# Forget gates inside the first stage, four projection chunks ahead of attention, two branch weights and gate chunks at its end, zero rows from another tile

## The chip, the core and the metric

The kernel runs on one core of a Trainium2 chip. Its time is the device time of one execution in microseconds (us), and lower is better. The core has five engines that run their own instruction streams: TensorE (PE, with its weight loads as PEld), VectorE (DVE), ScalarE (ACT), GpSimd (POOL) and SyncE (SP), which here issues nearly all DMA transfers. Each engine takes its instructions in the order in which they stand in its stream; semaphores order the streams against each other.

## What is computed

One layer of an encoder block on 1024 tokens of width 1024, all in float32:

```
z   = rms_norm(x) @ W_in          # q/k/v + forget logits (8), q/k/v of the second attention, 2 x 1024 gates
a   = forgetting attention         # 8 heads of 64, causal; scores + F_q - F_k, F = cumsum(log_sigmoid(ff + b))
b   = differential attention       # 4 heads, two score sets each, bias of distance, rms_norm of the result
y   = sigmoid(g_a) * (a @ W_pa) + sigmoid(g_b) * (b @ W_pb)
x   = x + y @ W_o
x   = x + two-of-32 expert layer(rms_norm(x))
out = rms_norm(x)
```

Every float32 matrix product is made of three matmuls: each operand is split into a high part, rounded to the matmul's format, and the low rest, and hi·hi, hi·lo and lo·hi are summed in PSUM.

## The kernel before

Five stages follow one another, and what matters here is how they meet.

- **Stage 1** (`stage_z1`, to about 118 us): norm of the eight token tiles, transposes, then the value columns and the forget logits in four column chunks (`values(c, t)`, c = 0..3; the logits come with c = 1). `stage_forget` follows as a piece of its own: log-sigmoid on ACT and DVE, a cumulative sum over tokens as twelve matmuls `pf` against a triangle `tri`, the result `t1` stored to the scratch tensor `fscr`. Its tiles are in pools that open after stage 1's have closed.
- **Projection chunks** (`z2_chunk`): 32 chunks of 128 columns, in the order q/k of the first attention (8), q/k of the second (8), gates (16). A chunk loads its weights (`zraw`), splits them (`zhi` on ACT, `zlo` on POOL), and makes 16 *pieces* of three matmuls into `pz`. After each half of a chunk ACT and DVE evict it (`sh`, `sl`) and four DMAs write q or k to scratch; gates get one. `fill(n)` emits n pieces. The first 2 chunks (32 pieces) run ahead of attention.
- **Attention** (`pipeline`): 8 heads of the first kind, then 4 of the second, eight query tiles (steps) each. A step makes scores (`ps`), DVE adds the bias and takes the maximum (`te`), ACT exponentiates, DVE scales, PE transposes (`pt`), ACT and DVE evict the transposed probabilities as high and low part (`PT`), PE multiplies with the values (`po`). Pieces of the projection are spread between these as filling, by weight i + 1.5 for step i: 256 in all for the first kind, 224 for the second.
- **Branches** (`branches(hb)`, from about 740 us): the attention outputs come back from scratch (`o`), the two branch weights are loaded in eight column groups (`praw`), split (`phi`, `plo`), multiplied (`pj`), gated, summed; then the output product, norm and routing by tiles.
- **Experts** (from about 981 us): 32 experts whose weights are streamed, and the final norm.

Around the change the PE order is the program's own (`manual_schedule`) from the first projection chunk to the end of attention. The other engines' streams, SP's among them, and PE's in stage 1 and in the branches are set by a list scheduler when the program is built, which takes instructions by priority as soon as its own clock says that they are ready; a DMA can thus stand far ahead of its place in the program. The zero rows of `ys` (2048 rows into which the experts' results are scattered) are one such case: `ys_clear` stands after attention in the program, its 16 DMAs from the tile `zero` stand in SP's stream in stage 1, from 37.6 to 77 us.

Buffers come from pools that are stacked; a tile of a new pool waits for the old tiles whose place it takes.

Of the kernel before, what the change touches and what calls it, by code (L numbers as in the profile page):

```python
# [8 lines left out]
F32 = mybir.dt.float32  # L9
# [42 lines left out]
class Block:  # L52
# [77 lines left out]
    def stage_z1(self):  # L130
# [4 lines left out]
        with ExitStack() as st:  # L135
# [67 lines left out]
            for t in range(NT):  # L203
                norm(t)
                if t + 4 < NT:
                    load_x(t + 4)
                if t == 3:
                    nc.sync.dma_start(self.bff, self.bcast(a["b_fgate"]))
                    load_w(1)
                values(0, t)  # L210
            for c in range(1, 4):
                if c + 1 < 4:
                    load_w(c + 1)
                for t in range(NT):
                    values(c, t)


    def stage_forget(self):
        nc = self.nc
        self.fscr = self.dram("fscr", [FOX_H, S], F32)  # L220
        with ExitStack() as st:
            p = self.pool(st, "fg")
            pp = self.pool(st, "pfg", space=PSUM)
            x = self.ffall.rearrange("p t h -> p (t h)")
            n = NT * FOX_H
            ab = p.tile([128, n], F32, name="ab")
            nc.scalar.activation(ab, x, AF.Abs)
            nc.scalar.activation(ab, ab, AF.Exp, scale=-1.0)
            nc.scalar.activation(ab, ab, AF.Ln, bias=1.0)
            lf = p.tile([128, n], F32, name="lf")  # L230
            nc.vector.scalar_tensor_tensor(lf, x, 0.0, ab, op0=OP.min, op1=OP.subtract)
            st_ = p.tile([128, NT, 64], F32R, name="lfs")
            nc.vector.memset(f32(st_), 0.0)
            l3 = lf.rearrange("p (t h) -> p t h", t=NT)
            nc.vector.tensor_copy(st_[:, :, 0:8], l3)
            nc.vector.tensor_tensor(st_[:, :, 32:40], l3, f32(st_[:, :, 0:8]), op=OP.subtract)
            ji = p.tile([128, S], I32, name="ji")
            nc.gpsimd.iota(ji, pattern=[[1, S]], base=0, channel_multiplier=-1)
            tri = p.tile([128, S], F32R, name="tri")
            nc.vector.tensor_scalar(tri, ji, 0.0, None, op0=OP.is_ge)  # L240
            ps = pp.tile([64, S], F32, name="pf")
            for hb in range(2):
                js = [j for j in range(NT) if j * 128 < (hb + 1) * 512]
                for j in js:
                    k0 = max(hb * 512, j * 128)
                    nc.tensor.matmul(ps[:, k0:(hb + 1) * 512], st_[:, j], tri[:, k0 - j * 128:(hb + 1) * 512 - j * 128],
                                     start=(j == 0), stop=(j == js[-1]))
            t1 = p.tile([8, S], F32, name="t1")
            nc.scalar.activation(t1, ps[32:40], AF.Copy)
            nc.vector.scalar_tensor_tensor(t1, ps[0:8], -1.0, t1, op0=OP.mult, op1=OP.subtract)  # L250
            nc.sync.dma_start(self.fscr, t1)


    def z2_setup(self, st):
# [9 lines left out]
        self.zero = self.pool(st, "zz", side="right").tile([128, 512], F32, name="zero")  # L264
        self.nc.gpsimd.memset(self.zero, 0.0)
# [57 lines left out]
    def z2_all(self):  # L323
# [6 lines left out]
        self.fill(2 * 2 * KC)  # L330
# [247 lines left out]

    def proj_setup(self, sa, sb, sw):
# [3 lines left out]
        self.opp = self.pool(sa, "op", 1)  # L583
        self.wpp = self.pool(sa, "wp", 2)
        self.tpp = self.pool(sa, "tpp", 2)
# [33 lines left out]

    def branches(self, hb):  # L620
# [3 lines left out]
        O = [self.opp.tile([128, KC, 512], F32R, name=f"o{s}") for s in range(2)]  # L624
        for br_ in range(2):
            for s in range(2):
                nc.sync.dma_start(f32(O[s][:, 4 * br_:4 * br_ + 4]),
# [636 lines left out]
```

## Time and profile before

| | |
|---|---|
| median of 3 runs | 1620.63 us (1620.57 to 1621.64) |
| profiled execution | 1615.66 us, span 1613.8 us |
| PE busy | 1493.0 us, 93% of the span |
| DVE, ACT, POOL busy | 1048.1, 882.5, 288.8 us |
| mean granted PE clock | 0.971 |
| stage 1 / chunks and forget / attention | to 118.5 / to 158.2 / to 722.5 us |
| gap and branches, first half | 722.5 to 740.0 / to 786 us |

A row of the timeline is start, duration, engine, line, operation, output<-input, shape and count; in brackets stands how long the engine had been idle before it, and what it waited for. `L305` is line 305 of the kernel. PEclk is the share of the full TensorE clock that was granted. A row of windows has the stretch, its length, the busy time (with the number of instructions) of PE, PEld, DVE, ACT and POOL, then PEclk, the share of DMA and GB/s.

### The profile page before, as it was taken

What the parts mean: (1) busy time and instruction counts of PE and PEld (TensorE: products, weight loads), DVE (VectorE), ACT (ScalarE), POOL (GpSimd) and SP (SyncE); (2) the same over time, 40 slices, a digit from 0 to 9 for tenths busy, and PEclk for the clock granted to TensorE, in tenths of its full rate; (3) what the DMA queues carried; (4) which work ended last, traced back from release to release, by engine and by line L of the source; (5) the groups of instructions that cost most, each with busy time, mean ns of one, the idle gap of its engine ahead of it and who ended that gap; (6) DMA issues with size and microseconds to landing.
All of it is one profiled execution on the core that took longest, in us unless ns stands there. A gap on an engine that the chain in (4) does not pass through costs nothing.

```text
span 1613.8 us, 21890 instructions
## 1 busy us (share of the span) xinstructions
PE 1493.0 (93%) x7713; PEld 1174.4 (73%) x7713; DVE 1048.1 (65%) x1926; ACT 882.5 (55%) x1327; POOL 288.8 (18%) x278
## 2 busy tenths in 40 slices
PE   6996999999999999996999959999999998999996
PEld 6994777777788888885888846666667666666663
DVE  6112555555555545545657459999999888888966
ACT  5212444444454444433312138878888877777764
POOL 2301122222221321210020131131011111111014
PEclk9998999999999999998999979999999999999998
DMA  8927566666644544349934759999999999999936
GB/s 267 332 96 236 139 179 171 164 161 162 159 134 129 166 151 131 111 148 248 313 112 144 313 202 337 377 354 368 385 376 375 374 344 356 346 350 342 351 133 253
DMA packets 181284, 394.94 MB, mean 245 GB/s; under 512 B 21714, under 2 KB 99538, under 8 KB 156594
## 3 DMA queue, kind: packets, MB, share of 16 engines
q1 hardware_dynamic: 174114, 376.89, 69.3%
q0 software_dynamic: 7056, 16.62, 3.1%
q8 instruction: 61, 1.00, 0.3%
q14 instruction: 53, 0.43, 0.1%
HBM read 324.36 MB, written 77.25 MB: 249 GB/s over the span
## 4 chain that ended last, share of the span: by engine, by line
PE 79%; DVE 8%; DMA 6%; issue 4%; ACT 2%; SPq 1%; POOL 1%; ACTq 0%; DVEq 0%; POOLq 0%
PE pz L305 7%; PE pz L306 7%; PE pz L307 7%; PE m L980 6%; PE m L981 6%; PE m L979 6%; PE mpy L1013 3%; PE mpy L1011 3%; PE mpy L1012 3%; DVE mlo L46 3%; PE po L472 2%; PE pt L386 2%; PE ps L360 2%; PE ps L361 2%; DMA mraw<-in_w_dram 2%
## 5 line engine op out<-in xcount | busy, mean ns | idle before, releaser
L46 DVE TENSOR_TENSOR mlo<-mraw,mhi 128x1024 fp32r<-128x1024 f32 x384 | 450.1, 1219 | 40.5 <-ACT mhi L45 38.7
L45 ACT ACTIVATE mhi<-mraw 128x1024 fp32r<-128x1024 f32 x384 | 391.7, 1056 | 64.3 <-PE m L981 46.6
L980 PE MATMUL m<-mlo,XT 128*96 128x512 f32 x512 | 205.6, 402 | 22.3 <-DVE mlo L46 22.3
L305 PE MATMUL pz<-ht,zhi 128*128 128x512 f32 x512 | 215.6, 421 | 0.0
L979 PE MATMUL m<-mhi,XT 128*96 128x512 f32 x512 | 206.5, 403 | 0.0
L981 PE MATMUL m<-mhi,XT 128*96 128x512 f32 x512 | 205.1, 401 | 0.0
L307 PE MATMUL pz<-ht,zlo 128*128 128x512 f32 x512 | 202.5, 396 | 0.0
L306 PE MATMUL pz<-ht,zhi 128*128 128x512 f32 x512 | 201.3, 393 | 0.0
L369 ACT ACTIVATE te<-te,nm 128x256 f32<-128x256 f32 (+7 forms) x128 | 99.2, 775 | 145.1 <-DVE nm L365 145.1
L980 PEld LDWEIGHTS m<-mlo,XT 128*96 128x96 f32 x512 | 84.3, 165 | 64.8 <-DVE mlo L46 31.0
L365 DVE CUSTOM_DVE_ANT_0 te<-ps,nF 128x512 f32<-128x512 f32 (+3 forms) x128 | 75.0, 588 | 76.8 <-PE ps L361 48.6
L46 DVE TENSOR_TENSOR PT<-pt,PT 128x512 fp32r<-128x512 f32 (+1 forms) x144 | 77.0, 554 | 73.3 <-ACT PT L45 71.4
L277 POOL TENSOR_TENSOR zlo<-zraw,zhi 128x1024 fp32r<-128x1024 f32 x32 | 76.7, 2398 | 209.9 <-ACT zhi L276 208.9
L307 PEld LDWEIGHTS pz<-ht,zlo 128*128 128x128 f32 x512 | 96.7, 189 | 21.9
L45 ACT ACTIVATE PT<-pt 128x512 fp32r<-128x512 f32 (+1 forms) x144 | 66.4, 488 | 84.2 <-PE pt L386 57.6
L981 PEld LDWEIGHTS m<-mhi,XT 128*96 128x96 f32 x512 | 84.1, 164 | 35.4 <-issue 0.5
L979 PEld LDWEIGHTS m<-mhi,XT 128*96 128x96 f32 x512 | 84.3, 165 | 34.4 <-issue 0.6
L305 PEld LDWEIGHTS pz<-ht,zhi 128*128 128x128 f32 x512 | 98.4, 192 | 13.5
L306 PEld LDWEIGHTS pz<-ht,zhi 128*128 128x128 f32 x512 | 97.7, 191 | 13.6
L1013 PE MATMUL mpy<-mhi,GT 128*96 128x512 f32 x256 | 101.7, 397 | 2.8 <-DVE GT L46 2.5
L1011 PE MATMUL mpy<-mhi,GT 128*96 128x512 f32 x256 | 102.3, 400 | 0.6 <-ACT GT L45 0.6
L1012 PE MATMUL mpy<-mlo,GT 128*96 128x512 f32 x256 | 100.4, 392 | 0.0
(263 smaller groups left out, 2797.1 us busy)
## 6 DMA issues: line engine op xcount, KB each, us to landing
mraw<-in_w_dram SPq DMA_DIRECT2D x192, 1024.0 KB, 8.1
zraw<-in_w_in_dram SPq DMA_DIRECT2D x32, 512.0 KB, 4.3
ys<-zero SPq DMA_DIRECT2D x16, 512.0 KB, 4.9
gscr<-sh SPq DMA_DIRECT2D x32, 256.0 KB, 2.0
o<-oscr SPq DMA_DIRECT2D x8, 1024.0 KB, 7.5
g<-gscr SPq DMA_DIRECT2D x32, 256.0 KB, 4.5
mraw<-ys SPq DMA_DIRECT2D x8, 1024.0 KB, 10.9
xt<-in_x_dram SPq DMA_DIRECT2D x8, 512.0 KB, 5.0
```

The source lines that it names most:

```text
L45: nc.scalar.activation(hi, src, AF.Copy)
L46: nc.vector.tensor_tensor(lo, src, f32(hi), op=OP.subtract)
L305: nc.tensor.matmul(ps, hi[:, k], self.hT[0][:, k, tk], start=(k == 0), stop=False)
L306: nc.tensor.matmul(ps, hi[:, k], self.hT[1][:, k, tk], start=False, stop=False)
L307: nc.tensor.matmul(ps, lo[:, k], self.hT[0][:, k, tk], start=False, stop=(k == KC - 1))
L369: nc.scalar.activation(t[:, :n], t[:, :n], AF.Exp, scale=-1.0, bias=nm, accum_out=rs)
L979: nc.tensor.matmul(ps, XT[0][:, k], hi, start=(k == 0), stop=False)
L980: nc.tensor.matmul(ps, XT[0][:, k], lo, start=False, stop=False)
L981: nc.tensor.matmul(ps, XT[1][:, k], hi, start=False, stop=(k == KC - 1))
L1011: nc.tensor.matmul(ps[n], GT[0][:, k], hi[:, nn], start=(k == 0), stop=False)
L1012: nc.tensor.matmul(ps[n], GT[0][:, k], lo[:, nn], start=False, stop=False)
L1013: self.last_down = nc.tensor.matmul(ps[n], GT[1][:, k], hi[:, nn], start=False, stop=(k == 3))
```

## The change

Five things move.

1. `stage_forget` becomes a generator inside stage 1, with stage 1's pools. Its first half (log-sigmoid, the triangle, now 640 wide) is emitted after `values(2, 0)`, its second (the matmuls in two groups, eviction in two halves, the store to `fscr`) after `values(2, 4)`. The cleared `lfs` moves from DVE to POOL.
2. 64 pieces (4 chunks) run ahead of attention in place of 32.
3. The filling of attention is 224 pieces for the first kind and 200 for the second; the 24 pieces that are left stand after attention.
4. Attention's pools close when its pipeline ends. Then `proj_first` opens the pools of the branch weights and loads the weights of the first two column groups and the first part of `o`, ahead of the 24 pieces in the program.
5. The zero rows come from `yroom` (cleared at setup by POOL) in whole 4 KB rows, emitted four each in the norm of the tiles 0 to 3; the tile `zero` is gone.

```
-            self.stage_forget()
-            self.att_setup(st)
             with self.tc.manual_schedule(engines={mybir.EngineType.PE}):
-                self.z2_all()
...
-                self.pipeline(share(fox, 16 * KC * 2 - 4 * KC + 32) + share(diff, 14 * 2 * KC))
-                self.fill(16 * KC)
-            self.ys_clear()
+                with ExitStack() as sh:
+                    self.att_setup(sh)
+                    self.z2_all()
...
+                    self.pipeline(share(fox, 14 * 2 * KC) + share(diff, 12.5 * 2 * KC))
+                sa = ExitStack()
+                self.proj_first(sa)
+                self.fill(2 * 2 * KC)
...
-        self.fill(2 * 2 * KC)
+        self.fill(4 * 2 * KC)
...
+            forget = self.stage_forget(gp, pp)
             for c in range(1, 4):
...
                 for t in range(NT):
                     values(c, t)
+                    if c == 2 and t in (0, 4):
+                        next(forget)
...
+    def proj_first(self, sa):
+        self.wpp = self.pool(sa, "wp", 2)
+        self.opp = self.pool(sa, "op", 1)
+        self.tpp = self.pool(sa, "tpp", 2)
+        self.bw = {j: self.branch_weights(j) for j in range(2)}
+        self.O = self.branch_rows()
+        self.load_o(0, 0)
...
+    def branch_weights(self, j):
+        nc, a = self.nc, self.a
+        n = slice(j * 128, (j + 1) * 128)
+        raw = self.wpp.tile([128, KC, 128], F32, name="praw")
+        hi = self.wpp.tile([128, KC, 128], F32R, name="phi")
+        lo = self.wpp.tile([128, KC, 128], F32R, name="plo")
+        nc.sync.dma_start(raw[:, 0:4], a["w_pa"][0].rearrange("(c p) n -> p c n", p=128)[:, :, n])
+        nc.sync.dma_start(raw[:, 4:8], a["w_pb"][0].rearrange("(c p) n -> p c n", p=128)[:, :, n])
+        split(nc, hi, lo, raw)
+        return hi, lo
...
+        if t < NT // 2:
+            for i in range(4):
+                self.ys_clear(4 * t + i)
...
-        nc.vector.memset(f32(st_), 0.0)
+        nc.gpsimd.memset(f32(st_), 0.0)
...
-        tri = p.tile([128, S], F32R, name="tri")
+        tri = p.tile([128, 640], F32R, name="tri")
...
-    def ys_clear(self):
+    def ys_clear(self, t):
-        self.ys = self.dram("ys", [2 * S, D], F32)
-        for t in range(2 * NT):
-            self.nc.sync.dma_start(self.ys[t * 128:(t + 1) * 128].rearrange("p (k n) -> p k n", k=2),
-                                   self.zero.unsqueeze(1).to_broadcast([128, 2, 512]))
+        self.nc.sync.dma_start(self.ys[t * 128:(t + 1) * 128], self.yroom)
```

How the streams move, at three places.

SP's stream from the store of the forget sums to the first load of `kk` (the keys of head 0), before: the store waits for `t1` and stands ahead of the keys, with parts of q and the values between.

```order
L275 DMA zraw<-in_w_in_dram 128x8x128
L399 DMA qq<-qscr_f 128x512
L251 DMA fscr<-t_1388 8x1024
L401 DMA qq<-qscr_f 64x512
L402 DMA qq<-qscr_f 64x512
L456 DMA v<-vscr_f 128x8x128
L392 DMA kk<-kscr_f 128x1024
```

Now the store (L255) stands in stage 1, among the stores of the values, and the keys of head 0 come after the stores of the third chunk's first half, while a chunk and a half of matmuls are still ahead of attention:

```order
L322 DMA kscr_f<-sh 64x512
L323 DMA kscr_f<-sl 64x512
L453 DMA nF<-fscr 128x1024
L322 DMA qscr_f<-sh 64x512
L323 DMA qscr_f<-sl 64x512
L322 DMA qscr_f<-sh 64x512
L323 DMA qscr_f<-sl 64x512
L395 DMA kk<-kscr_f 128x1024
```

What moved is the store, out of the way of the keys, and the four stores of one more half chunk, ahead of them.

ACT's stream where the first head gives way to the second (`te` 128x1024 is the last step's exponential, `te` 128x128 the next head's first), before:

```order
L369 ACTIVATE te,rs<-te,nm 128x1024
L45 ACTIVATE PT_1915<-pt 128x3x128
L45 ACTIVATE PT_1914<-pt 128x4x128
L276 ACTIVATE zhi<-zraw 128x1024
L369 ACTIVATE te,rs<-te,nm 128x128
L45 ACTIVATE sh<-pz 128x512
L45 ACTIVATE PT_1914<-pt 128x4x128
L45 ACTIVATE PT_1915<-pt 128x4x128
```

and now:

```order
L372 ACTIVATE te,rs<-te,nm 128x1024
L45 ACTIVATE sh<-pz 128x512
L45 ACTIVATE PT_2038<-pt 128x3x128
L45 ACTIVATE PT_2037<-pt 128x4x128
L372 ACTIVATE te,rs<-te,nm 128x128
L45 ACTIVATE PT_2037<-pt 128x4x128
L45 ACTIVATE PT_2038<-pt 128x4x128
```

The split `zhi` and the eviction `sh` have left this place. Before, 32 pieces per head put a chunk's end at every change of heads, and all seven changes read alike. With 28 pieces the place wanders: the changes 1, 2, 5 and 6 have no `zhi` there, 3 and 7 have it ahead of the `PT` evictions, and the fourth, like the change to the second attention, reads as before. On PE one piece in place of two stands between the last head's transposes and the new head's first.

ACT's stream at the end of attention, now (`PT` of the last two query tiles, which the last products wait for):

```order
L372 ACTIVATE te,rs<-te,nm 128x1024
L412 ACTIVATE ohi<-ot 128x512
L45 ACTIVATE phi<-praw 128x1024
L45 ACTIVATE PT_7346<-pt 128x3x128
L45 ACTIVATE phi<-praw 128x1024
L45 ACTIVATE PT_7345<-pt 128x4x128 x2
L45 ACTIVATE PT_7346<-pt 128x4x128
```

and SP's at the same place:

```order
L637 DMA praw<-in_w_pa_dram 128x4x128
L638 DMA praw<-in_w_pb_dram 128x4x128
L637 DMA praw<-in_w_pa_dram 128x4x128
L415 DMA oscr_1387<-ohi 128x512
L415 DMA oscr_1388<-olo 128x512
L638 DMA praw<-in_w_pb_dram 128x4x128
```

Before, both `phi` stood after the last `PT` and the last `ohi`, and no load of `praw` stood ahead of the store of that `olo`. Now the two splits stand between the last evictions (the two `plo` likewise on DVE), and the second weights' second half is issued after the store of `olo`, the low part of the output of the half before the last; on POOL a `zlo` has come to stand ahead of that `olo`. The 16 stores of zero rows stand in SP's stream between the second and the sixth head of the first attention.

More of the change, by code (lines that the diff above doesn't have):

```diff
@@ L215, in stage_z1, with stage_forget @@
                     values(c, t)
-    def stage_forget(self):
+                    if c == 2 and t in (0, 4):
+                        next(forget)
+    def stage_forget(self, p, pp):
         nc = self.nc
         self.fscr = self.dram("fscr", [FOX_H, S], F32)
[L221 to L232, printed above, removed]
-            nc.vector.memset(f32(st_), 0.0)
[L234 to L238, printed above, removed]
-            tri = p.tile([128, S], F32R, name="tri")
[L240 to L251, printed above, removed]
@@ new lines, in stage_forget @@
+        x = self.ffall.rearrange("p t h -> p (t h)")
+        n = NT * FOX_H
+        ab = p.tile([128, n], F32, name="ab")
+        nc.scalar.activation(ab, x, AF.Abs)
+        nc.scalar.activation(ab, ab, AF.Exp, scale=-1.0)
+        nc.scalar.activation(ab, ab, AF.Ln, bias=1.0)
+        lf = p.tile([128, n], F32, name="lf")
+        nc.vector.scalar_tensor_tensor(lf, x, 0.0, ab, op0=OP.min, op1=OP.subtract)
+        st_ = p.tile([128, NT, 64], F32R, name="lfs")
+        nc.gpsimd.memset(f32(st_), 0.0)
@@ new lines, in stage_forget @@
+        l3 = lf.rearrange("p (t h) -> p t h", t=NT)
+        nc.vector.tensor_copy(st_[:, :, 0:8], l3)
+        nc.vector.tensor_tensor(st_[:, :, 32:40], l3, f32(st_[:, :, 0:8]), op=OP.subtract)
+        ji = p.tile([128, 640], I32, name="ji")
+        nc.gpsimd.iota(ji, pattern=[[1, 640]], base=0, channel_multiplier=-1)
+        tri = p.tile([128, 640], F32R, name="tri")
+        nc.vector.tensor_scalar(tri, ji, 0.0, None, op0=OP.is_ge)
+        yield
+        t1 = p.tile([8, S], F32, name="t1")
@@ new lines, in stage_forget @@
+        for hb in range(2):
+            ps = pp.tile([128, 4, 128], F32, name="pt", bufs=4).rearrange("p a b -> p (a b)")[:64]
+            js = [j for j in range(NT) if j * 128 < (hb + 1) * 512]
+            for j in js:
+                k0 = max(hb * 512, j * 128)
+                w, o = (hb + 1) * 512 - k0, min(k0 - j * 128, 128)
+                nc.tensor.matmul(ps[:, k0 - hb * 512:], st_[:, j], tri[:, o:o + w], start=(j == 0), stop=(j == js[-1]))
+            c = slice(hb * 512, (hb + 1) * 512)
+            nc.scalar.activation(t1[:, c], ps[32:40], AF.Copy)
+            nc.vector.scalar_tensor_tensor(t1[:, c], ps[0:8], -1.0, t1[:, c], op0=OP.mult, op1=OP.subtract)
@@ L254, in z2_setup @@
+        nc.sync.dma_start(self.fscr, t1)
+        yield
     def z2_setup(self, st):
@@ L1220, in run @@
                 sw = sb.enter_context(ExitStack())
-                with ExitStack() as sa:
+                with sa:
                     self.proj_setup(sa, sb, sw)
```

37 lines of the change are left out of this document (17 added, 20 removed).

## The prediction

> **What bounds the kernel now.** I read the page first, then PE's waits, then the windows around the longest of them, then the timeline at both ends of attention.
>
> ```profile
> span 1613.8 us, 21890 instructions
> PE 1493.0 (93%) x7713; PEld 1174.4 (73%) x7713; DVE 1048.1 (65%) x1926; ACT 882.5 (55%) x1327; POOL 288.8 (18%) x278
> ```
>
> PE is busy for 93% of the span, so a gain is either PE work that disappears, and this change removes none worth the name, or PE time that is waited away or runs at a reduced clock. The waits of PE, where the columns are the sum in us, the count and the longest:
>
> ```profile
> PE pt L386 <- DVE PT L46: 15.3, 8, 2.2
> PE pj L644 <- ACT phi L45: 12.5, 1, 12.5
> PE ps L360 <- DMA kk<-kscr_f: 10.2, 1, 10.2
> PE pf L246 <- DVE lfs L236: 5.4, 1, 5.4
> ```
>
> These four are 43.4 us, all between 139 and 740 us, and all at places where the change works. The windows show a second loss beside the waits:
>
> ```profile
> 139.00:158.20 19.20, 3.69 (x12) 2.22 (x12) 3.15 (x6) 5.53 (x8) 3.28 (x2) 0.72 0.77 216
> 158.20:164.00 5.80, 5.77 (x18) 4.52 (x19) 2.42 (x11) 1.26 (x5) 0.00 (x0) 0.50 1.06 338
> 318.00:357.00 39.00, 37.30 (x200) 30.99 (x198) 22.18 (x56) 18.15 (x37) 8.81 (x12) 0.96 0.61 160
> 740.00:744.40 4.40, 4.36 (x10) 2.97 (x11) 2.36 (x2) 1.66 (x2) 0.00 (x0) 0.50 1.16 316
> 744.40:786.00 41.60, 40.02 (x176) 32.79 (x175) 34.80 (x43) 18.96 (x22) 0.00 (x0) 1.00 1.00 283
> ```
>
> After the two long waits the granted clock is 0.50 for 5.8 and 4.4 us, although PE is busy all the time. Within a head of attention (318 to 357 us) PE has 37.3 of 39.0 us, DVE 22 and ACT 18: PE sets the pace there, and the 2 us that are missing are one wait.
>
> **Start of attention: two waits go.**
>
> ```profile
> 144.31 3.69 PE L246 MATMUL pf<-tri,lfs 128*64 128x512 f32 x12 [5.37 <-DVE lfs L236]
> 150.32 0.33 SPq L251 DMA_DIRECT2D fscr<-t  x1
> 152.54 0.51 SPq L392 DMA_DIRECT2D kk<-kscr_f  x1
> 158.23 0.55 PE L360 MATMUL ps<-kk,qq 128*128 128x256 f32 x1 [10.23 <-DMA kk<-kscr_f]
> ```
>
> The forget sums now stand four value tiles behind their inputs, which are ready long before: 5.37 us go. The twelve matmuls stay, but in a stream that never stops; at the full clock in place of the 0.72 of this window I take 2.1 us for 3.69, a gain of 1.6 us. The keys were issued at 152.54 because SP had waited for `fscr` until 150.32. Now they are issued with a chunk and a half of projection still to come. One projection half is eight pieces, and a piece (three matmuls of 512 columns) takes 0.65 to 0.67 us by the spacing inside attention; 24 pieces are 16 us, against the 5.7 us from issue to first use here. So 10.23 us go, and with the wait the half clock behind it: half of 5.8 us, taken as 2.8. The two chunks that move ahead cost nothing, because they are taken from attention's filling. What would undo this is an SP queue that reaches the keys late; it has 16 us of cover and four half-chunk stores ahead of it.
>
> **Changes of heads: most of a wait goes.** The 15.3 us are 2.1 us at each of seven changes of heads, plus 0.3. The fourth:
>
> ```profile
> 352.48 1.06 ACT L276 ACTIVATE zhi<-zraw 128x1024 fp32r<-128x1024 f32 x1 [0.76 <-PE pz L306]
> 353.62 2.39 POOL L277 TENSOR_TENSOR zlo<-zraw,zhi 128x1024 fp32r<-128x1024 f32 x1 [1.70 <-ACT zhi L276]
> 354.37 1.73 DVE L461 TENSOR_SCALAR te<-te,rs 128x128 f32<-128x128 f32 x1
> 357.44 0.30 PE L386 MATMUL pt<-ident,te 128*128 128x128 f32 x1 [2.14 <-DVE PT L46]
> ...
> 161.44 0.29 DVE L461 TENSOR_SCALAR te<-te,rs 128x128 f32<-128x128 f32 x1
> ```
>
> The scaling of a 128-wide `te` takes 0.29 us in head 0 and 1.73 here, ending when POOL's `zlo` ends (356.01). ACT's `zhi`, 1.06 us, stands ahead of the exponential that feeds it. Both are there because 32 pieces per head put a chunk's end at every change. With 28, changes 1, 2, 5 and 6 have no `zhi`, 3 and 7 have it earlier: there 1.06 + 1.44 us leave the chain, while the one piece less between the transposes (0.65 us) shortens the cover. 2.14 + 0.65 - 2.5 is 0.3 us; in changes 2 and 6 the eviction `sl` keeps about 0.7 us in the chain, so I take 1.0. Change 4 becomes 2.14 + 0.65 = 2.8. Sum: 4 x 0.3 + 2 x 1.0 + 2.8 = 6.0 in place of 15.0, a gain of 9; I take 8, since `zlo` now meets `te` inside the heads. There the slack is large:
>
> ```profile
> 347.95 0.75 DVE L461 TENSOR_SCALAR te<-te,rs 128x1024 f32<-128x1024 f32 x1
> 352.52 1.04 PE L386 MATMUL pt<-ident,te 128*128 128x128 f32 x8
> ```
>
> The scaled row is ready at 348.70 and is wanted at 352.52: 3.8 us, of which the thinner filling takes one piece. In the second attention I allow 1 us at the three changes, where no wait of note shows now. Bounds: 0 to 13 us for the first, 0 to 3 us of loss for the second.
>
> The Trainium skill (SBUF — State Buffer, section "Who interferes with whom") says that GpSimd and VectorE share a port pair as an exclusive lock, so a VectorE `tensor_scalar` in a fast mode waits for the whole GpSimd instruction. By that rule the trace's 1.73 us are the lock, and the trace agrees. The rule also speaks against this change: a `zlo` now falls on the last query tile's score combination, below.
>
> **End of attention: one wait goes, one comes.**
>
> ```profile
> 711.31 2.31 POOL L410 TENSOR_TENSOR olo<-ot,ohi 128x512 fp32r<-128x512 f32 x1 [11.99 <-ACT ohi L409]
> 713.65 0.32 SPq L412 DMA_DIRECT2D oscr<-olo  x1
> 717.00 0.60 ACT L45 ACTIVATE PT<-pt 128x512 fp32r<-128x512 f32 x1 [3.09 <-PE po L541]
> 717.46 0.60 PE L386 MATMUL pt<-ident,te 128*128 128x128 f32 x4
> 719.81 2.66 PE L541 MATMUL po<-PT,v 128*128 128x256 f32 x21
> 727.44 0.35 SPq L595 DMA_DIRECT2D gmoe<-in_g_moe_dram  x1
> 734.50 0.43 SPq L636 DMA_DIRECT2D praw<-in_w_pb_dram  x1
> 738.82 1.06 ACT L45 ACTIVATE phi<-praw 128x1024 fp32r<-128x1024 f32 x1 [10.17 <-DMA praw<-in_w_pb_dram]
> 739.91 1.23 DVE L46 TENSOR_TENSOR plo<-praw,phi 128x1024 fp32r<-128x1024 f32 x1 [3.83 <-ACT phi L45]
> 739.93 0.80 PE L644 MATMUL pj<-o,phi 128*128 128x512 f32 x1 [12.49 <-ACT phi L45]
> 766.47 0.50 PE L646 MATMUL pj<-o,plo 128*128 128x512 f32 x1 [1.58 <-DVE plo L46]
> ...
> DMA to landing us min/median/max: 2.8/4.9/7.1
> ```
>
> PE waits 12.49 us because the second half of the first weight is issued at 734.50, behind loads that need room at 727.44 and behind the last store. Now two weights are split before attention's last product, and 24 pieces, 16 us, lie between that product's norm and the branches; the reload of `o` and the gates are issued under them. So 12.49 us go, and 2.2 us of half clock behind them (half of 4.40). The later 1.58 us, a `plo` behind a late load, I count as gone too: the loads start earlier against the matmuls.
>
> What comes: ACT must do the second `phi` before it may evict `PT` (717.00), and that weight's second half is issued only after the store of `olo`, issued at 713.65 here. With a `zlo` (2.39 us) ahead of this `olo` on POOL the issue falls near 716.0 + 0.4; landing takes 2.8 us at least, giving 719.2; `phi` 1.06 and `plo` 1.23, which stands ahead of `PT`'s low part on DVE, give 721.5, and that part (0.69 us) 722.2. Only then can PE start the transposes that start at 717.46 here: a stall of 4.7 us, counted as 5 with the clock. Behind it wait the last products, the norm and its store, all 24 pieces, everything. Bounds: 0 if the weights land before the `PT` are due, 7 with the median landing of 4.9 us.
>
> The Trainium skill (TensorE: Matmul & The Clock Gate, section "What's actually happening") has the clock halve after an idle window of about 3.4 us; by that this stall would also cost some 1.7 us of half clock behind it, and the sum would be that much smaller. The trace agrees where it idles for 10 and 12 us; an idle stretch of 5 us inside attention no row shows.
>
> **Zero rows.** Their 16 DMAs leave SP's queue in stage 1 and come back between the second and sixth heads, 8 MB more where the DMA share is 0.61 (window 318 to 357). The loads there are issued a half head or more ahead, so I price them at nothing; without that cover each would cost a landing. Stage 1 gains 0 to 2 us of freer transfers; I take 0.5.
>
> **The sum** against the profiled span: -5.4 - 1.6 - 10.2 - 2.8 (start) - 8 + 1 (attention) + 5 - 12.5 - 2.2 - 1.6 (end) - 0.5 = -38.8 us, so 1575.0 us span. The profiled execution took 1615.66, 5 us under the median of 1620.63; taking the difference to the median gives 1581.8, say **1582 us**.
>
> **Rivals.** (a) The changes of heads keep their waits, because the chain there is longer than I read it: without the 8 us, 1590. For it: a piece less of cover; against: the 1.73 us. (b) The weights land in time and the end does not stall: 1577. Against it: the order of the streams. (c) A wait of similar kind comes back at one end, the keys behind SP's stores or the gates behind `gmoe`: 10 us less, 1592. (d) Slower: attention is paced by its chain and not by PE. Then the 32 + 24 pieces taken out of it, 37 us of PE work, do not shorten it but are paid again outside. The certain gains (5.4 + 1.6 + 10.2 + 2.8 + 12.5 + 2.2 + 1.6 = 36.3) then stand against 37 and the 5 us stall: +6, 1627. It decides once more than 31 of the 37 us are not recovered. The 3.8 us of slack and DVE's 22 of 39 us speak against it.
>
> **Chances.** Forecast 0.55, (a) 0.20, (b) 0.13, (c) 0.07, (d) 0.05. Low end: every bound on the good side, 5 at the end, 5 at the heads and 1 in stage 1 more, about 1571. High end: (a) with (c) half come true, 1597. A change within 0.2%, 3 us, is one that these runs can't tell from none: 0.02. Faster 0.94, slower 0.04.
>
> **What would show it.** Right: no wait at `pf` and the first `ps`, granted clock 1.00 there; waits of `pt` on `PT` near 6 us in all; a PE gap of about 5 us before the last transposes with ACT waiting for `praw`; no gap before `pj`. Wrong: heads of attention as long as before (39 us) with PE idle in them, which is (d), or a gap at `ps` or `pj` on `kk`, `o` or `g`, which is (c).

## The result and the profile after

The changed kernel takes 1571.08 us (median of 4 runs, 1569.67 to 1575.55) against 1621.11 us for the kernel before on the same chip (1620.57 to 1621.64): a ratio of 0.9696, with an interval of 0.9676 to 0.9716. That is 50.0 us less by the medians. Forecast were 1582 us with a range of 1571 to 1597: the sign and most of the places are right, the gain is 11 us larger, and the time lies at the very low edge of the range; that it still lies inside is luck. The profiled executions, on which the sum was made, go from 1615.66 to 1570.37 us, their spans from 1613.8 to 1568.6: 45.2 us against the 38.8 of the sum. So some 6 us of the difference are in the terms, and the rest is in the step from the profiled execution to the median, which was 5 us before and is 0.7 us now.

The first part of the page, and then rows of PE's waits (sum, count, longest):

```profile
span 1568.6 us, 21877 instructions
PE 1483.5 (95%) x7713; PEld 1167.3 (74%) x7713; DVE 1050.8 (67%) x1926; ACT 881.6 (56%) x1328; POOL 289.4 (18%) x279
```

```profile
PE pt L389 <- DVE PT L46: 6.7, 4, 2.8
PE pv L183 <- DVE vs L46: 1.7, 1, 1.7
PE pj L670 <- DVE plo L46: 0.5, 1, 0.5
```

Of the four waits that were 43.4 us, three have no row any more, and the fourth is 6.7 in place of 15.3: 4.4 at the changes of heads (forecast: "near 6 us in all") and 2.3 at the end of attention (forecast as a gap of about 5). PE's busy time fell too, by 9.5 us with the same 7713 matmuls; the mean granted clock is 0.983 in place of 0.971. The timeline of PE and SP where the first two waits were:

```profile
86.28 2.25 PE L251 MATMUL pt<-tri,lfs 128*64 128x512 f32 x12
150.21 0.59 SPq L395 DMA_DIRECT2D kk<-kscr_f  x1
163.21 0.28 PE L363 MATMUL ps<-kk,qq 128*128 128x256 f32 x1
694.38 0.39 PE L668 MATMUL pj<-o,phi 128*128 128x512 f32 x1
```

The twelve sums run without a wait, in 2.25 us. The keys are issued 13 us before the first scores, and neither the first `ps` nor the first `pj` has a bracket. The way along the span, where "net" takes off the 32 pieces (21.3 us in the trace of before) that now run ahead of attention:

| place | before, us | after, us | net gain | sum of the prediction up to there |
|---|---|---|---|---|
| first scores | 158.23 | 163.21 | 16.4 | 17.7 |
| first `pj` of the branches | 739.93 | 694.38 | 45.6 | 35.0 |
| first transpose of an expert's inputs | 959.75 | 912.22 | 47.5 | 38.8 |
| end of the span | 1613.8 | 1568.6 | 45.2 | 38.8 |

The start came within 1.3 us of the sum. Between the first scores and the branches 29.2 us were gained where 17.3 were forecast: this is where the terms were wrong.

### The profile page after: what moved, and what is told of

Same layout as the page of the kernel before. It is cut to its first block, busy times and chain, and to the rows that moved or that the text cites. A ratio compares the mean times of both kernels' runs of the same rounds, so it can differ in the third digit from the quotient of the medians.

```text
span 1568.6 us, 21877 instructions
## 1 busy us (share of the span) xinstructions
PE 1483.5 (95%) x7713; PEld 1167.3 (74%) x7713; DVE 1050.8 (67%) x1926; ACT 881.6 (56%) x1328; POOL 289.4 (18%) x279
## 4 chain that ended last, share of the span: by engine, by line
PE 81%; DVE 6%; DMA 5%; issue 3%; ACT 2%; SPq 1%; POOL 0%; DVEq 0%; ACTq 0%; POOLq 0%
PE pz L308 7%; PE pz L310 7%; PE pz L309 7%; PE m L1008 6%; PE m L1009 6%; PE m L1007 6%; PE mpy L1041 3%; PE mpy L1039 3%; PE mpy L1040 3%; PE pt L389 3%; DMA mraw<-in_w_dram 3%; DVE mlo L46 3%; PE po L475 3%; PE ps L363 2%; PE ps L364 2%
## 5 line engine op out<-in xcount | busy, mean ns | idle before, releaser
L985 POOL DMA_INDIRECT X<-h,sg x32 | 39.2, 1226 | 327.3 <-PE mpt L995 320.3
```

## The experiments

Each kernel is the changed kernel with one edit, unless it says otherwise. The column "against" is the median less 1571.08 us; kernels of other rows ran on other chips, where the kernel before took 1618.5 to 1621.1 us, so differences under some 3 us are read from the traces, not from this column.

| kernel | median, us | ratio to before, interval | against |
|---|---|---|---|
| changed | 1571.08 | 0.9696 (0.9676 to 0.9716) | |
| two chunks ahead | 1584.22 | 0.9778 (0.9757 to 0.9799) | +13.1 |
| 32 pieces a head | 1588.91 | 0.9804 (0.9788 to 0.9820) | +17.8 |
| forget gates back | 1574.17 | 0.9716 (0.9699 to 0.9732) | +3.1 |
| cover at the end gone | 1585.30 | 0.9781 (0.9765 to 0.9798) | +14.2 |
| splits behind the evictions | 1573.51 | 0.9721 (0.9695 to 0.9747) | +2.4 |
| weights late | 1579.33 | 0.9758 (0.9731 to 0.9784) | +8.3 |
| 66 ahead | 1565.60 | 0.9677 (0.9650 to 0.9704) | -5.5 |
| thin second attention | 1578.38 | 0.9752 (0.9725 to 0.9778) | +7.3 |
| 68 ahead, 32 a head | 1566.01 | 0.9675 (0.9660 to 0.9690) | -5.1 |
| zero rows ahead of attention | 1593.58 | 0.9848 (0.9833 to 0.9863) | +22.5 |
| 66 ahead, one load from ACT | 1562.27 | 0.9651 (0.9638 to 0.9664) | -8.8 |
| zero rows in stage 1 | 1573.95 | 0.9728 (0.9708 to 0.9749) | +2.9 |

The first four undo one part each. Their losses add up to 48.2 us, near the whole 50.0, but that they do is partly chance: the 3.1 us of the forget gates are lost at another place than theirs (below), and the two parts at the start overlap.

### Changes of heads: the share, or the place of the chunk's end?

**32 pieces a head.**

```diff
-                    self.pipeline(share(fox, 14 * 2 * KC) + share(diff, 12.5 * 2 * KC))
+                    self.pipeline(share(fox, 256) + share(diff, 168))
```

> Only the share of a head of the first attention is undone: 256 pieces there in place of 224 and 168 in the second in place of 200, 64 ahead and 24 at the end as in the changed kernel. Theory 1 (the waits at the changes of heads come from a chunk's end that falls on the change): seven waits of 2.1 to 2.8 us, 15 to 19 us in all in place of 4.4, and half clock behind three or four of them, 5 to 6 us in place of 1.6: +12 to +20 us, about 1587. Theory 2 (the waits shrank because less projection work, and less of its eviction, meets the chain): the waits stay near 4.4 us or fall with the thicker cover: -1 to +3 us. Theory 3 (the pace is the chain's, so the second attention is shorter by what it has less to do and the first is longer): the heads of the first attention keep their 30 to 36 us.

Measured: +17.8 us, and the seven waits are back. Of PE's waits between 160 and 600 us, first in this kernel, then in the changed one:

```profile
PE pt L389 <- DVE PT L46: 14.7, 7, 2.5
```

```profile
PE pt L389 <- DVE PT L46: 4.4, 3, 2.8
```

So the 28 pieces a head are worth 10.3 us of waits, and most of the rest is not wait but clock: four stretches at half clock behind waits of heads in place of one, 1.7 us each (last section). Two more kernels tell whether it is the number or the place.

**66 ahead**, and **68 ahead with 32 a head**:

```diff
-        self.fill(4 * 2 * KC)
+        self.fill(66)                    # the other: 68
...
+                    self.pipeline(share(fox, 224) + share(diff, 198))   # the other: 256 and 164
```

> 66 pieces ahead of attention in place of 64, 224 in the first attention as in the changed kernel, 198 in place of 200 in the second: the changes of heads then stand 14, 10, 6, 2, 14, 10 and 6 pieces into a chunk, so none meets a chunk's end (0) or its middle (8). Theory 1 (a wait at a change needs a chunk's end, 2.1 to 2.8 us, or a half's eviction, 0.78 us, at that place): the 2.82 and the two 0.78 us go, with the 1.6 us of half clock behind the first: -4 to -6 us against the changed kernel, about 1566. Theory 2 (the fourth change has another cause, or the two pieces are too few to pass the splits by): the waits move or stay, -1 to +2 us.

> 68 pieces ahead, 256 in the first attention (32 a head, as in the kernel before), 164 in the second, 24 behind. Every change of heads then stands 4 pieces into a chunk. Theory 1 (only the place of the chunk's end against the change counts, not how many pieces a head has): no wait of over 1 us at any of the seven changes, no half clock behind them, and a time near that of the kernel with 66 pieces ahead: about 1566. Theory 2 (32 pieces a head are what made the waits): they are back as in the run with 64 ahead and 32 a head, about 1588.

Measured: 1565.6 and 1566.0 us. The intervals of both overlap the changed kernel's, so the gain in time is not clear of noise; that in waits is plain. In the first, PE's only waits between 160 and 600 us are these; in the second the list is empty.

```profile
PE pt L389 <- DVE te L464: 1.7, 3, 0.7
```

The place decides, not the number: with 32 a head the waits are 14.7 us when a chunk ends on every change, and none when every change stands 4 pieces into a chunk. The change's 28 helped because the seven changes then stand 12, 8, 4, 0, 12, 8 and 4 pieces into a chunk: six of seven chunk ends are away from them. What stands at the fourth change, where one is left, in the changed kernel (ACT, POOL, DVE, PE):

```profile
297.03 1.06 ACT L279 ACTIVATE zhi<-zraw 128x1024 fp32r<-128x1024 f32 x1 [0.76 <-PE pz L309]
298.17 2.38 POOL L280 TENSOR_TENSOR zlo<-zraw,zhi 128x1024 fp32r<-128x1024 f32 x1 [1.70 <-ACT zhi L279]
298.92 1.71 DVE L464 TENSOR_SCALAR te<-te,rs 128x128 f32<-128x128 f32 x1
300.55 0.68 DVE L49 SCALAR_TENSOR_TENSOR sl<-pz,sh 128x512 fp32r<-128x512 f32 x1
301.98 0.30 PE L389 MATMUL pt<-ident,te 128*128 128x128 f32 x1 [2.82 <-DVE PT L46]
```

It is the picture that the prediction read in the kernel before: a 128-wide `te` takes 1.71 us and ends with `zlo` (300.55), and 2.82 us are lost, as forecast (2.8). How much of that is `te` beside `zlo`, and how much `zhi` ahead of the exponential, no kernel here separates.

### Start of attention

**Two chunks ahead.**

```diff
-        self.fill(4 * 2 * KC)
+        self.fill(32)                    # and 56 pieces behind attention
```

> Only the part on chunks ahead of attention is undone: 32 pieces ahead in place of 64, and the 32 pieces stand at attention's end with the 24 (56 there); the phase of the chunk ends against the changes of heads stays (32 more or less is two whole chunks). Theory 1 (the keys need cover by projection work): head 0's keys are in the second chunk, whose last piece now ends where attention begins; eviction 1.5 us, store 2.1 us and load 5.7 us follow it, so PE waits 8 to 9 us at the first scores and runs some 5 us at half clock behind it: +10 to +12 us against the changed kernel, about 1582. Theory 2 (the keys waited in the kernel before because SP stood at the store of the forget sums, which is now far ahead): +0 to +3 us, about 1572.

Measured: +13.1 us. The keys, then the first scores:

```profile
146.87 0.37 SPq L395 DMA_DIRECT2D kk<-kscr_f  x1
153.13 0.55 PE L363 MATMUL ps<-kk,qq 128*128 128x256 f32 x1 [10.84 <-DMA kk<-kscr_f]
```

Theory 1: the wait is 10.84 us although the store of the forget sums is long done (issued at 90.58). The keys need the work ahead of them. Its size is 2 us over the estimate: SP has four stores and one load of its own to issue between the last piece (142.3) and the keys.

**Forget gates back.** `stage_forget` is again the function of the kernel before, with pools of its own.

```diff
-                    if c == 2 and t in (0, 4):
-                        next(forget)
...
             self.diff_bias()
+            self.stage_forget()
```

> Only the forget part is undone: log-sigmoid, triangle and sums stand behind stage 1 in pools of their own, as in the kernel before, where the twelve sums now come after about 37 of the 64 pieces. Theory 1 (the wait belongs to the pools, whose tiles become free only when stage 1 is over): the wait on lfs is back with 3 to 5.4 us and the sums take 2.2 to 3.7 us; the keys keep some 25 pieces of cover behind the store, so they cost nothing: +4 to +7 us, about 1577. Theory 2 (the store of the sums is what held the keys): both waits are back, +14 to +18 us, about 1587.

```profile
142.86 2.30 PE L246 MATMUL pf<-tri,lfs 128*64 128x512 f32 x12 [1.09 <-DVE lfs L236]
```

Measured: +3.1 us; in the span 3.4, less than either theory. The keys are not waited for, so theory 2 falls. With more pieces ahead, the sums fall later and their wait is only 1.09 us. On the other hand stage 1 ends at 116.6 us here and at 119.8 in the changed kernel. So at the first scores the two differ by 0.25 us only (163.46 and 163.21): once four chunks stand ahead of attention, moving the forget part gains next to nothing there. The rest arises behind them: 1.2 us in head 0, where PE waits 1.81 us for `te` in place of 0.60, and 4.6 us of half clock at the end of attention, of which 2.5 us come back later, in code that is the same. At that end the wait before the last transposes (2.41 us here) lies whole in one stretch of 3.41 us, and half clock follows (in a row of windows the first number behind the comma is PE's busy time, the third from the end the clock):

```profile
668.39:671.80 3.41, 1.00 (x9) 0.74 (x8) 2.42 (x3) 1.87 (x3) 0.00 (x0) 1.00 1.15 297
671.80:675.21 3.41, 3.41 (x18) 3.41 (x17) 0.69 (x1) 0.60 (x1) 0.00 (x0) 0.50 0.89 213
```

Two more stretches at half clock follow from 678.62 on, and the changed kernel has none there. That is a matter of where its waits happen to fall (last section), and no merit of the change.

In stage 1 the forget part costs 3.2 us, not the 2.25 of its sums. It brought a wait that the prediction did not have (POOL, DVE, DVE, PE of the changed kernel):

```profile
71.72 4.74 POOL L160 TENSOR_TENSOR wlo<-wraw,whi 128x1024 fp32r<-128x1024 f32 x2 [18.44 <-ACT whi L159]
74.62 1.92 DVE L232 SCALAR_TENSOR_TENSOR lf<-ffall,ab 128x64 f32<-128x64 f32 x1 [3.40 <-ACT ab L230]
76.68 0.88 DVE L46 TENSOR_TENSOR vs<-pv,vs 128x256 fp32r<-128x256 f32 x1
77.64 0.39 PE L183 MATMUL pv<-whi,ht 128*128 128x256 f32 x1 [1.68 <-DVE vs L46]
```

`lf`, 64 columns, took 0.23 us at its old place. Here it starts under POOL's `wlo` and ends with it (76.46); the evictions of the values queue behind it, and PE waits 1.68 us. (The difference of the two stages is smaller than 2.25 + 1.68, since stage 1 of the kernel with the gates back has 0.9 us more of other waits.)

### End of attention

**Cover gone.**

```diff
-                    self.pipeline(share(fox, 14 * 2 * KC) + share(diff, 12.5 * 2 * KC))
+                    self.pipeline(share(fox, 224) + share(diff, 224))
```

> The 24 pieces between attention and the branches go back into the second attention (224 there in place of 200, none behind it); the early weights and the early reload of o stay. Theory 1 (the pieces hide the norm of the last product and the reload of o): the reload takes the place of v and is issued when the last product ends, 8.7 us to landing, and the norm's own small waits lie in the same stretch: PE waits 6 to 12 us in sum between the last product and the first pj and runs some 2 us at half clock behind it: +6 to +13 us, about 1580. Theory 2 (the early weights alone removed the 12.5 us): +0 to +2 us, about 1572.

Measured: +14.2 us, with the weights early and split as before. Two waits on `o`, 1.27 us and 11.46 us, in sum a little over the estimate:

```profile
701.90 0.33 SPq L415 DMA_DIRECT2D oscr<-olo  x1
704.50 2.50 SPq L615 DMA_DIRECT2D gcol<-in_g_moe_dram  x1
708.14 0.98 SPq L647 DMA_DIRECT2D o<-oscr  x2
715.38 1.19 PE L668 MATMUL pj<-o,phi 128*128 128x512 f32 x2 [11.46 <-DMA o<-oscr]
```

The reload of the second branch's rows needs the last store (701.90), and SP issues it only 6 us later, behind six loads of the router's and the norm's constants. So the 24 pieces hide a store, a piece of SP's queue and a reload, and without them the old 12.5 us are back under another name.

**Weights late.**

```diff
-        self.bw = {j: self.branch_weights(j) for j in range(2)}
+        with self.tc.issue_after(self.last_store.ins):
+            self.bw = {j: self.branch_weights(j) for j in range(2)}
```

> The changed kernel, with the loads of the two early branch weights held behind the store of attention's last olo in SyncE's order, so that they are issued after attention's last product. Theory 1 (the 24 pieces hide everything at this end, and early weights are worth nothing beside them): landing takes 5 us, the splits 2.3, against 12 us of pieces that are left behind that store: no wait at the first pj, and the stall of 2.3 us before the last transposes is gone as well: -2 to -4 us against the changed kernel, about 1568. Theory 2 (the early weights are what removed the 12.5 us): a wait of 5 us or more at the first pj, +2 to +8 us, about 1576.

Measured: +8.3 us; both theories miss. The last product ends 1.3 us earlier and the first `pj` starts at 694.72 without a wait, as theory 1 has it. But with the weights the order on SP moved: the gates' first loads, issued at 690.33 us in the changed kernel, now stand behind the router's constants, at 701.39, and PE waits 3.67 us for `g` from 703.40 and 1.49 us for a `plo` from 713.71.

**Splits behind the evictions.**

```diff
+        with self.tc.issue_after(self.last_hi.ins), self.tc.issue_after(self.last_lo.ins):
             self.bw = {j: self.branch_weights(j) for j in range(2)}
```

> The changed kernel, with the splits of the two early branch weights (phi on ScalarE, plo on VectorE) held behind the last eviction of PT in both engines' order; the loads stay where they are. Theory 1 (the stall between the last transposes comes from splits that stand ahead of the evictions and wait for a weight's second half): the 2.3 us gap before the last transposes goes, and with it a part of the 1.2 us by which the evictions before it are late: -2 to -4 us against the changed kernel, about 1568; no new wait at the first pj, since 16 us of pieces lie in between. Theory 2 (the stall is the eviction's own chain, whatever stands ahead): 0, about 1571.

In the changed kernel the stall of the forecast is there: SP, ACT, DVE, PE.

```profile
663.05 0.34 SPq L415 DMA_DIRECT2D oscr<-olo  x1
663.44 0.43 SPq L638 DMA_DIRECT2D praw<-in_w_pb_dram  x1
666.66 1.06 ACT L45 ACTIVATE phi<-praw 128x1024 fp32r<-128x1024 f32 x1 [2.07 <-DMA praw<-in_w_pb_dram]
667.75 1.23 DVE L46 TENSOR_TENSOR plo<-praw,phi 128x1024 fp32r<-128x1024 f32 x1 [1.80 <-ACT phi L45]
669.63 0.66 PE L389 MATMUL pt<-ident,te 128*128 128x128 f32 x4 [2.30 <-DVE PT L46]
```

With the splits behind the evictions the gap is gone and the last product ends at 671.96 in place of 673.27. Yet the time does not fall (+2.4 us, intervals overlap). Rows of windows and of PE's timeline say where the gain went:

```profile
671.71:675.12 3.41, 1.38 (x12) 1.09 (x10) 0.94 (x2) 1.17 (x2) 1.01 (x1) 1.00 0.69 224
675.12:678.53 3.41, 3.41 (x12) 3.09 (x13) 0.69 (x1) 0.12 (x1) 0.00 (x0) 0.50 1.04 398
```

```profile
707.71 0.50 PE L671 MATMUL pj<-o,phi 128*128 128x512 f32 x1 [1.96 <-ACT phi L45]
```

The small waits of the norm, 0.69 and 1.34 us, which are in both kernels, now fall into one stretch and are followed by half clock. And the third weight, whose buffer is the first's, is loaded from 671.38 on in place of 665.50, so that `pj` waits 1.96 us for its split. What was late next was the third weight.

**66 ahead, one load from ACT.** On top of the kernel with 66 ahead, the load of the second weight's second half is issued from ACT's queue.

```diff
-        self.bw = {j: self.branch_weights(j) for j in range(2)}
+        self.bw = {j: self.branch_weights(j, nc.scalar if j else nc.sync) for j in range(2)}
```

> 66 pieces ahead and 198 in the second attention, and the second half of the second early weight is issued from ScalarE's queue, behind ohi, so that it no longer stands behind the store of olo on SyncE; splits and all else as in the changed kernel. Theory 1 (the stall of 2.3 us before the last transposes is the wait for that half, issued some 2 us late): the gap falls under 1 us, and since the split is not put off, the third weight is not late at the branches: -1.5 to -3 us against the same kernel with its load on SyncE (1565.6), about 1563. Theory 2 (splits ahead of the evictions cost what they cost, wherever the load is issued, or what is gained is given back in the branches): 1564 to 1567.

Measured: 1562.27 us. The stall, first with 66 ahead alone, then here:

```profile
664.03 1.11 PE L389 MATMUL pt<-ident,te 128*128 128x128 f32 x4 [2.28 <-DVE PT L46]
```

```profile
663.13 0.66 PE L389 MATMUL pt<-ident,te 128*128 128x128 f32 x4 [1.36 <-DVE PT L46]
```

The gap falls by 0.9 us, not under 1, and the spans of the two profiled executions are both 1560.4 us; against the kernel with 66 ahead the gain is not clear (the intervals overlap). Against the changed kernel it is (0.9638 to 0.9664 against 0.9676 to 0.9716): by its median this is the fastest kernel of the study.

### What sets the pace of a head

**Thin second attention.**

```diff
+                    self.pipeline(share(fox, 224) + share(diff, 136))   # 88 pieces behind attention
```

> 136 pieces in the second attention in place of 200, and 88 behind attention in place of 24: 16 pieces, 10.7 us of TensorE work, are taken out of each of its heads. Theory 1 (TensorE sets the pace there and the chain of softmax has slack): a head falls from 58 to about 48 us and the time stays within 3 us of the changed kernel's. Theory 2 (the paced-by-its-chain rival): the heads keep 55 us or more with TensorE idle in them, and up to 43 us are paid twice: 1600 to 1614.

Measured: the heads fall to between 45.8 and 48.9 us (their first 128-wide exponentials start at 439.35, 485.12, 532.57 and 581.51 us; in the changed kernel they are 55.7 to 58.1 us apart). PE is busy for all of the first stretch below, and from 445 to 629 us it has one wait of over 0.4 us (1.20 at 557.45):

```profile
480.00:530.00 50.00, 50.00 (x296) 43.48 (x295) 32.83 (x98) 28.52 (x59) 14.63 (x16) 1.00 0.52 164
626.00:640.00 14.00, 9.30 (x55) 8.33 (x55) 4.25 (x5) 4.75 (x7) 0.35 (x1) 0.76 0.87 226
640.00:645.00 5.00, 3.66 (x16) 3.29 (x16) 0.85 (x2) 0.00 (x0) 1.01 (x1) 0.66 0.95 356
```

So the rival of a chain that sets the pace is wrong here even with a third of the filling taken out of the second attention. The kernel still loses 7.3 us: the thinner last head has waits of 4.0 us before its last product in place of 2.3, and two times half clock follows (6.8 us from 631.27 and 3.4 us from 641.51).

### The zero rows

**Zero rows ahead of attention.**

```diff
+            for i in range(2 * NT):
+                self.ys_clear(i)
             with self.tc.manual_schedule(engines={mybir.EngineType.PE}):
```

> Only the zero rows' place is undone: the 16 writes come from the same cleared tile but stand ahead of the projection in the program, so that SyncE can issue them in stage 1 as in the kernel before. Theory 1 (they are free in either place): within 1.5 us of the changed kernel, 1570 to 1573, and stage 1 ends at most 1 us later. Theory 2 (they took part of what the first loads and stores of stage 1 need): +2 to +4 us, with longer waits of TensorE in stage 1.

Measured: +22.5 us, which neither theory allows. The writes did not move to stage 1; ten of them stand in one row on SP just ahead of the stores of the third chunk:

```profile
139.50 11.75 SPq L1069 DMA_DIRECT2D ys<-ylast  x10
151.35 1.21 SPq L322 DMA_DIRECT2D qscr_f<-sh  x1
...
158.31 0.80 PE L308 MATMUL pz<-ht,zhi 128*128 128x512 f32 x1 [15.67 <-DVE sl L46]
```

The eviction tiles `sh` and `sl` wait for their stores, and PE for the tiles. So the price of these rows is one of place: 15.7 us of wait here and half clock behind it. By the first scores 18.9 us are lost (182.12 in place of 163.21); a wait of 1.37 us for `qq` and two stretches at half clock at the end of attention follow. Inside the heads, where the change has them, no wait of PE is theirs.

**Zero rows in stage 1**, as in the kernel before.

```diff
+        self.zero = self.pool(st, "zz", side="right").tile([128, 512], F32, name="zero")
+        self.nc.gpsimd.memset(self.zero, 0.0)
...
+                for t in range(2 * NT):       # behind attention in the program
+                    self.ys_clear(t)          # 16 writes from zero
```

> The changed kernel with the zero rows as in the kernel before: the tile zero, cleared at setup, and 16 writes that SyncE issues in stage 1 from about 38 to 77 us. The run before this one put them right ahead of attention instead, where ten in a row held the stores of the second and third chunk back for 11.8 us (TensorE idle for 15.7 us). Theory 1 (in stage 1 nothing waits for what stands behind them): stage 1 ends within 1 us of 119.8, no new wait at the first scores, and the time is within 2 us of the changed kernel's, 1570 to 1573. Theory 2 (8 MB of writes cost wherever other transfers are due): stage 1 ends 1.5 us later or more, 1573 to 1577.

Measured: 1573.95 us, with stage 1 ending at 122.7 us in place of 119.8, as theory 2 has it; the time alone does not tell it from the changed kernel. PE starts 2.3 us later and has a wait of 2.21 us from 44.6 us that was in the kernel before too; the order of DVE's first instructions moved with the tile, so how much of it is the transfers stays open.

## Why the prediction was right, and where it was not

- **Start, 17.7 us forecast, 16.4 gained.** Both waits went, but only half of the mechanism holds. The step has the keys late "because SP had waited for `fscr`"; with that store long done and two chunks ahead the wait on `kk` is 10.84 us, and with the store late and four chunks ahead there is none. The cover of pieces decides, as the step's second half says, and the forget part's move adds 0.25 us beside it. The sums take 2.25 us (taken: 2.1). What is missing is the 1.68 us behind `lf`; the step "four value tiles behind their inputs, which are ready long before" looked at PE and not at what the new DVE instructions do to the evictions there. Stage 1 made up for it: taken at 0.5 us, it gained some 1.7 (it ended at 117.62 by its last `pv`, not at the 118.5 of the table ahead, and now ends at 119.83 with 3.93 us of forget part in it). PE starts at 8.28 us in place of 10.26, and its wait of 2.18 us before 45.84 has become 0.49; with the zero rows back in stage 1 both are nearly as before (10.55 and 2.21).
- **Changes of heads, 8 forecast.** The waits fell from 15.0 to 4.4 us, 10.6, within the bounds of 0 to 13. Per change the forecast was 0.3, 1.0, 0.3, 2.8, 0.3, 1.0 and 0.3; measured are none, 0.78, none, 2.82, none, 0.78 and none.
- **What the step left out is the clock.** "The 2 us that are missing are one wait" stands under a row whose clock is 0.96. Of the kernel before, four waits of heads are each followed by 3.4 us at half clock (from 239.5, 318.0, 396.6 and 437.5 us), in the changed one only the fourth change's. That is three stretches less, 1.7 us each: 5.1 us of gain that the sum has not. It counted half clock behind the two long waits alone. At the end of attention the changed kernel is lucky besides: its waits there are followed by no half clock, and in eleven of the twelve other kernels some stretch between 640 and 715 us is at half (in part behind waits of their own).
- **The stall at the end, 5 forecast, 2.3 measured.** Mechanism, rows and order are as forecast; the size is half. The step let `zlo` put off `olo` by its whole 2.4 us; in the trace `zlo` (659.37 to 661.79) ends only 0.5 us after `ohi` is ready, so the load was issued 3.9 us ahead of the time at which PE wanted the transposes (663.44 and 667.33), and not 1.1; its landing took 3.2 us (taken: 2.8). The kernel with the splits moved shows that the stall was worth 1.3 us at the last product, and nothing in the end.
- **Wait on `pj`, 12.5 forecast, 12.5 gained.** But the step gave the early weights and the pieces together the credit, and for this wait the runs give it to the pieces: without them 14.2 us are lost with the weights early; with them and late weights the first `pj` does not wait, and a loss comes later, through SP's queue.
- **Behind the first `pj`, 3.8 forecast.** 2.0 us are gained up to the experts; of the 1.58 us for `plo`, 0.53 stay. Then 2.3 us are lost again in code that did not change (654.1 us from there to the end before, 656.4 after, 653.0 with 66 ahead). They are not lost in the experts: from their first gather to the last expert's transposes the changed kernel is 0.8 us quicker (606.5 in place of 607.3). The final norm behind them is 3.1 us slower. A stretch at half clock begins in it at 1528.29, while the nearest one before lay ahead of it, among the experts, at 1529.77; the stretch ahead of 1528.29 has no idle time, so what put the clock down there stays open. And PE waits 4.03 us for DVE in place of 3.02, behind a scaling of 2.91 us in place of 1.89: it starts sooner after a GpSimd addition began, and ends 1.1 us behind it either way (POOL and DVE, before and after):

```profile
1581.10 2.37 POOL L1184 TENSOR_TENSOR fx<-fx,mraw 128x1024 f32<-128x1024 f32 x1 [0.19 <-DMA mraw<-ys]
1582.67 1.89 DVE L1196 SCALAR_TENSOR_TENSOR mraw<-mraw,rfr,mraw 128x1024 f32<-128x1024 f32 x1
...
1535.41 2.38 POOL L1209 TENSOR_TENSOR fx<-fx,mraw 128x1024 f32<-128x1024 f32 x1 [0.19 <-DMA mraw<-ys]
1535.96 2.91 DVE L1221 SCALAR_TENSOR_TENSOR mraw<-mraw,rfr,mraw 128x1024 f32<-128x1024 f32 x1
```

- **Rest.** These differences (2.6 + 5.1 + 2.7 between the first scores and `pj`) are 10.4 of the 11.9 us by which that stretch was better than forecast. PE's windows over it, before and after, place the last 1.5 us:

```profile
158.23:739.93 581.70, 551.18 (x3009) 465.20 (x3009) 311.51 (x846) 267.70 (x545) 126.62 (x150) 0.98 0.55 152
163.21:694.38 531.17, 520.99 (x2913) 441.36 (x2912) 308.46 (x843) 264.80 (x541) 124.09 (x149) 1.00 0.63 185
```

Idle time fell from 30.5 to 10.2 us, 20.3 where 14.5 were forecast (8 + 12.5 - 5 - 1): 0.5 more than the heads and the stall explain, spread over small waits. The half clock costs half of 6.2 + 4 x 3.4 us before and of 3.4 us after, 8.2 less where 2.8 were forecast: 0.3 more than the three stretches. The last 0.7 us are matmul time: what went is 22.0 us, and 21.3 were taken for the 32 pieces.
- **From span to median.** The 5 us that were added came from one execution before against its three runs. In the changed kernel the same difference is 0.7 us. It is no constant of the kernel, and cost 4 us of the error. Thirty more executions of the kernel before took 1615.93 to 1622.94 us, the shortest at a mean granted clock of 0.971 and the longest at 0.965; the profiled one, at 1615.66, was shorter than all of them.
- **Rivals.** Rival (a), waits that stay, fell. Rival (b), no stall, was nearest to the time, for another reason. Of rival (c) nothing came. Rival (d) is contradicted by PE at 50.00 of 50 us with 16 pieces a head less in the second attention, and in the first by the kernel with 66 ahead, whose eight heads have three waits of 0.74 us at most. The upper end of the range, 1597, is 2 us above what its own terms give (1590 and half of 10). The zero rows, "I price them at nothing", were free where the change put them; the 22.5 us at another place show that this was a matter of place and not of size.

## What to carry to other kernels

Where work is spread between the steps of a pipeline, look at where its block ends fall against the changes of the other loop: two or four pieces of offset removed waits that the same amount of filling at another place had left. Work that is held back for the end of a stage must cover the whole chain of store, queue and reload there, and the queue is the part that changes when anything else is moved. And count a wait with what the clock does behind it, which can be nearly as much again (1.7 us behind 2.1).

## What the runs showed of the hardware

The granted clock changes on a fixed grid. In the kernel before, half clock begins at 143.96, 239.52, 318.04, 396.56, 437.52 and 731.04 us (worked out from windows of 2 us): the others come 28, 51, 74, 86 and 172 times 3.413 us after the first. Whether a stretch of the grid runs at half clock depends in the main on how long PE idled in the one before it, and a wait of 2.1 us suffices if all of it falls into one. The second and the third change of heads of the kernel before, each with the same 2.1 us wait, in windows on that grid:

```profile
236.11:239.52 3.41, 1.27 (x10) 0.96 (x9) 3.23 (x7) 1.18 (x4) 1.05 (x1) 1.00 0.53 112
239.52:242.94 3.42, 3.42 (x16) 3.02 (x15) 0.78 (x3) 0.59 (x1) 0.82 (x4) 0.50 0.98 225
...
273.66:277.07 3.41, 2.91 (x19) 2.17 (x17) 2.10 (x7) 3.32 (x8) 2.18 (x1) 1.00 0.43 127
277.07:280.49 3.42, 1.79 (x15) 1.82 (x16) 2.71 (x7) 0.34 (x2) 0.56 (x3) 1.00 0.65 138
```

The first wait lies whole in one stretch (busy 1.27 of 3.41), and the next runs at half; the other straddles the border, and nothing happens. Over the fourteen traces of this case, from 20 us on, all 122 stretches at full clock with 1.9 us of idle time or more were followed by half clock, and so were 10 of 3531 with less than 1.6 us and 5 of the 35 between. Six of those ten were fully busy, each at the first matmuls of the final norm; idle time alone does not explain them. So the small waits of a kernel have no fixed price. The grid does not start with the kernel: counted from the span's start, a border lies at 0.60 us in the kernel before and at 2.53 us in the changed one (worked out from 143.96 and 302.90). Two executions of one program may then differ by 1.7 us for each wait near this bound; that is an estimate, as only one execution of each kernel was traced.

The Trainium skill (TensorE: Matmul & The Clock Gate, section "What's actually happening") has a free-running activity window of 3413 ns, and the trace agrees with its length. The rule of the same page (section "HAM oscillation — how this bites in real kernels") that gaps over about 3.4 us are the ones to avoid is too mild by these rows: 2.1 us within one window were enough.

The second thing is how small an instruction can be and still stand behind GpSimd: 64 columns on VectorE took 1.92 us in place of 0.23 while a 2.4 us `wlo` ran. The Trainium skill (SBUF — State Buffer, section "Who interferes with whom") says that a VectorE instruction with two inputs in SBUF contends with a GpSimd instruction that reads SBUF, and the second to issue blocks for the whole of the first; the trace agrees, with `lf` ending 0.08 us behind `wlo`.
